# A hybrid decoder layer on one core: a second gate tile projected inside the first three token groups, with the next group's turns spread over more slices

## The chip, the cores and the metric

The kernel runs on one core of one Trainium2 chip. The metric is the device time of one execution in microseconds; lower is better. Several runs of the same kernel are timed and their median is given. One further execution is recorded by the hardware profiler, and all the views below come from it.

## The reference

One decoder layer over 2048 tokens of width 1024, batch 1. The input x is RMS-normalised and modulated (`h`), then projected by one wide matrix into queries, keys, values and gates of two attention branches:

```python
h = rms_norm(x, g_pre) * (1.0 + scale) + shift          # scale, shift, gate from silu(c) @ w_ada + b_ada
qa, ka, va, fa, za, qb, kb, vb, zb = split(h @ w_in)    # 512,512,512,8,512,512,128,128,512 columns
oa = forgetting_attention(qa, ka, va, fa + b_fgate) * silu(za)      # 8 heads, causal, forget-gate bias
ob = sliding_window_sink_attention(rope(qb), rope(kb), vb, sinks) * silu(zb)   # 8 query, 2 key heads, window 128
y = concat([oa, ob]) @ w_out
out = x + gate * rms_norm(y, g_post)
```

## The kernel before, in words

All large products are made of fp16 pairs: each operand is split into a high and a low half, and a product is three matmuls (high-high, high-low, low-high) for every 128 of the 1024 input columns. The tokens are worked on in four groups of 512 (`ci` 0 to 3, `NCH` = 4).

**The stages.** A start (lines 421 to 641) loads w_ada and the first x tiles, computes scale and shift, and from them the per-column factors `Gp` and `Shp` of the normalised x. `Gp` needs a bound over all columns: line 613 makes `bnd`, line 615 its maximum per partition (`bmx`), and lines 617 to 625 carry it over the partitions to `pH`, `Gp` and `Shp`. A prologue then projects the sliding-window keys and values of all four groups and prepares x group by group. The window stage goes through 32 windows of the sliding-window branch, the forgetting attention follows (8 heads, with the remaining projections between its steps), and the output projection ends the kernel.

**Turns.** x of a group is normalised (`squares` on ScalarE, line 372; `root` on VectorE, lines 92 to 106; `normal`, line 382 on ScalarE or 384 on VectorE), and then turned, 128 columns at a time: `turn_x(ci, k)` issues four transposes on TensorE (line 390), then ScalarE scales them by `Gp` and `Shp` (line 396, once or twice), and VectorE makes the low half (lines 400 and 401). The result, `hT[ci]`, is what every projection reads. Eight turns make a group.

**Slices.** Projection work is cut into units that stand in one list, `punits`, by `add(key, units)`. `kb` is the window keys, `vb` the window values, `qb0` to `qb3` the window queries, `zb0` to `zb3` the gates of the window branch (128 columns each), `va` the forgetting values. A unit of `kb`, `qb` or `zb` is three matmuls of 128x512 (line 307); a unit of `vb` is twelve of 128x136 (line 740); eight units are one key for one group. `fill(n)` (line 1024) takes the next n slices and runs, before each, what `events` has for that position. What comes after a product (copies out of PSUM, tanh, rotation) is put off by `after(n, f)` and run at the n-th `tick`, two slices apart in the prologue. Each engine works through its own instructions in order.

**Weights of a key.** When a key is first added, `add` enters eight events for it, so many slices ahead of its first unit: load by a DMA that GpSimd issues (`w_load`, line 205, 42 slices ahead), the maximum on VectorE (`w_max`, line 211, 31), a trip of the maxima through DRAM, again issued by GpSimd (lines 214 and 219, `mx_d` and `mxr`, 31 and 21), the common scale (`w_scale`, line 230, 12), the high half on ScalarE (line 245, 8), the low half on VectorE (line 251, 6 and 4), and the constants (`w_done`, 3). A position below zero becomes the event's number n (line 911), so load and maximum come no later than the slices 0 and 1. The raw weights lie in one of two buffers (`wraw`), the split ones of zb and va in one of two others (`whl`). kb and zb0 hold the raw buffers at first.

**The list before.** For each of the groups 0, 1 and 2: `kb`, `vb`, `zb0`, 24 units, with the eight turns of the next group behind the units of the list `at_` (line 947). Then kb and vb of group 3, qb0 of group 0, zb0 of group 3, qb0 of group 1 and zb1 of group 0. That is the prologue, `N_PRO` = 144 slices. The other 296 slices (14 of `qbs` and 23 of `others`, eight units each) are dealt out to the 32 windows (line 1061). A window is: maxima of the scores on VectorE (line 844), exps on ScalarE (line 855), transposes on TensorE (`turn`, line 864), the product with the values (line 883), and the scores of the next window (line 831), with slices between them.

**Rows that the prediction reads.** `wh_kb` (line 251) is the low half of kb's weights, `tz` a gate tile after its tanh (lines 351 and 347), `junk` the squares of x, `pxb` the transposes in a window, `hT<-in_x_dram` and `xt<-in_x_dram` the loads of x.

Of the kernel before, what the change touches and what calls it, by code (L numbers as in the profile page):

```python
# [24 lines left out]
NCH = S // CH  # L25
# [15 lines left out]
def hybrid_layer(  # L41
# [158 lines left out]
    def w_load(key, pieces, eng=None):  # L200
        width = VB if key == "vb" else P
        raw = (vbw if key == "vb" else wpool).tile([P, KT, width], F32, tag="wraw", name=f"wr_{key}")
        o = 0
        for col0, n in pieces:
            (eng or G).dma_start(raw[:, :, o:o + n], w_in0[:, col0:col0 + n].rearrange("(k p) n -> p k n", p=P))
            o += n
        wq[key] = [raw]

    def w_max(key):
        mx = sm(1, "w_mx")  # L210
        V.tensor_reduce(mx[:], wq[key][0][:], axis=AX.XY, op=ALU.max, apply_absolute_value=True)
        md = mx_d[len(kaps_seen) % 3]
        kaps_seen.append(key)
        G.dma_start(md[:], mx[:])
        wq[key].append(md)

    def w_back(key):
        mxr = mxp.tile([P, P], F32, tag="mxr", name="mxr")
        G.dma_start(mxr[:], wq[key].pop().rearrange("p o -> (p o)").partition_broadcast(P))
        wq[key].append(mxr)  # L220

    def w_scale(key):

        floor = key[:2] == "qk"
        raw, mxr = wq[key]
        if key in first:
            mx2 = mxr
        else:
            mx2 = sm(1, "w_mx2")
            V.tensor_reduce(mx2[:], mxr[:], axis=AX.X, op=ALU.max)  # L230
        pw = sm(1, "w_pw")
        pow2_floor(pw[:], mx2[:], "w_p2")
        if floor:
            V.tensor_tensor(pw[:], pw[:], pfl[:], op=ALU.max)
        sw = sm(1, "w_sw")
        V.reciprocal(sw[:], pw[:])
        V.tensor_scalar(sw[:], sw[:], 2.0 ** 14, None, op0=ALU.mult)
        wq[key] = [raw, pw, sw]

    def w_high(key):  # L240
        raw, pw, sw = wq[key]
        width = VB if key == "vb" else P
        pool = vbw if key == "vb" else wpq if key[0] in "qk" else wpool
        whl = pool.tile([P, 2, KT, width], F16, tag="whl", name=f"wh_{key}")
        A.activation(whl[:, 0], raw[:], AF.Identity, scale=sw[:])
        wq[key].append(whl)

    def w_low(key, part, parts=2):
        raw, pw, sw, whl = wq[key]
        ks = slice(KT * part // parts, KT * (part + 1) // parts)  # L250
        V.scalar_tensor_tensor(whl[:, 1, ks], raw[:, ks], sw[:], whl[:, 0, ks], op0=ALU.mult, op1=ALU.subtract)  # L251
        if part == parts - 1:
            wq[key] = whl
            pws[key] = pw
# [12 lines left out]
    def w_done(key):  # L267

        kind, j = key[:2], key[2:]
        pw = pws[key]  # L270
        if kind == "qk":
            kap = kappa(pw, key)
            scl[key] = col(f"scl_{key}")
            V.tensor_scalar(scl[key][:], kap[:], kap[:], 0.125, op0=ALU.mult, op1=ALU.mult)
            isc[key] = col(f"isc_{key}")
            V.reciprocal(isc[key][:], scl[key][:])
        elif kind == "qb":
            kap = kappa(pw, key)
            scl[key] = col(f"scl_{key}")
            V.tensor_scalar(scl[key][:], kap[:], kaps["kb"][:], 0.125, op0=ALU.mult, op1=ALU.mult)  # L280
        elif kind == "va":
            kaps[key] = kappa(pw, key)
        else:
            czs[key] = col(f"cz_{key}")
            V.tensor_scalar(czs[key][:], pw[:], pH[:], 2.0 ** -29, op0=ALU.mult, op1=ALU.mult)
            n = int(j) + (4 if kind == "zb" else 0)
            V.tensor_tensor(fac8[:, n:n + 1], kaps["vb" if kind == "zb" else f"va{j}"][:], czs[key][:], op=ALU.mult)

    def pieces(key):
        kind, j = key[:2], int(key[2:] or 0)  # L290
        if kind == "vb":
            return [(OFF_VB, P), (OFF_FA, 8)]
        if kind == "qk":
            return [(OFF_QA + j * 64, 64), (OFF_KA + j * 64, 64)]
        return [({"qb": OFF_QB, "kb": OFF_KB, "va": OFF_VA, "za": OFF_ZA, "zb": OFF_ZB}[kind] + j * P, P)]
# [71 lines left out]
    def squares(ci, us=range(4)):  # L367
        if ci not in rstd:
            rstd[ci] = sm(4, "ss"), sm(4, "rst")
        for u in us:  # L370
            junk = hst.tile([P, D], BF16, tag="junk", name="junk", bufs=1)
            A.activation(junk[:], xt[ci * 4 + u], AF.Square, accum_out=rstd[ci][0][:, u:u + 1])

    def root(ci):
        ss, rst = rstd[ci]
        rsqrt_mean(rst, ss[:], 4)

    def normal(ci, us=range(4)):
        for u in us:
            t, r = ci * 4 + u, rstd[ci][1][:, u:u + 1]  # L380
            if ci == 0 or (ci == 1 and u % 2):
                A.activation(xt[t], xt[t], AF.Copy, scale=r)
            else:
                V.tensor_scalar(xt[t], xt[t], r, None, op0=ALU.mult)
# [20 lines left out]
    def turn_x(ci, k):  # L405
        scaled, split = turn(ci, k)
        after(1, scaled)
        after(2, split)
# [309 lines left out]
    def kb_units(ci):  # L718
        cols_ = slice(ci * CH, (ci + 1) * CH)

        def finish(stg):
            for g in range(2):
                for h in range(2):
                    SP.dma_start(kst[g][64 * h:64 * h + 64, :, cols_], stg[64 * g:64 * g + 64, :, :])

        return proj_units("kb", ci, evac_rope(ci, finish, stp))
# [80 lines left out]
    def qb_units(j, ci):  # L807
        def finish(stg):
            ab[j, ci] = stg

        return proj_units(f"qb{j}", ci, evac_rope(ci, finish, None))
# [88 lines left out]
    def add(key, us):  # L900
        if key not in pkeys and key not in ("kb", "vb"):
            at = len(punits) - (24 if key[:2] == "za" else 0)
            for n, (lead, f) in enumerate(((42, lambda: w_load(key, pieces(key))), (31, lambda: w_max(key)),
                                           (21, lambda: w_back(key)), (12, lambda: w_scale(key)),
                                           (8, lambda: w_high(key)), (6, lambda: w_low(key, 0)),
                                           (4, lambda: w_low(key, 1)), (3, lambda: w_done(key)))):
                if key == "zb0":
                    if n >= 3:
                        events.setdefault(n + 9, []).append(f)
                else:  # L910
                    events.setdefault(max(at - lead, n), []).append(f)
        if key not in pkeys:
            pkeys.append(key)
        punits.extend(us)

    events = {}
    others = []
# [5 lines left out]
    def at_slice(n, f):  # L923
        events.setdefault(n, []).append(f)
# [14 lines left out]
    for ci in range(NCH):  # L939
        n0 = len(punits)  # L940
        add("kb", kb_units(ci))
        add("vb", vb_units(ci))
        if ci < 3:
            add(*others[ci])

            mine, punits[n0:] = punits[n0:], []
            at_ = [10, 12, 14, 16, 17, 18, 19, 20] if ci else [12, 14, 16, 17, 18, 19, 20, 21]
            for n, u in enumerate(mine):
                punits.append(u)
                if n in at_:  # L950
                    punits.append(lambda ci=ci, k=at_.index(n): turn_x(ci + 1, k))
            if ci:
                for u in range(4):
                    at_slice(n0 - 9 + 2 * u, lambda ci=ci, u=u: squares(ci + 1, (u,)))
                    at_slice(n0 + 3 + u, lambda ci=ci, u=u: normal(ci + 1, (u,)))
                at_slice(n0 + 2, lambda ci=ci: root(ci + 1))
            at_slice(n0 + 12, lambda ci=ci: spread(ci + 1))
            if ci < 2:
                at_slice(n0 + 12, lambda ci=ci: [load_x(t) for t in range(4 * ci + 8, 4 * ci + 12)])
# [1 line left out]
    at_slice(n0, lambda: open_fox())  # L961
    at_slice(n0 + 8, gates)
    add("qb0", qb_units(0, 0))
    add(*others[3])
    add("qb0", qb_units(0, 1))
    add(*others[4])
    N_PRO = len(punits)
    qbs = [(f"qb{c_ // 4}", qb_units(c_ // 4, c_ % 4)) for c_ in range(2, 16)]
    n_o = 5
    for n, (key, us) in enumerate(qbs):  # L970
        add(key, us)
        lim = 5 + 5 * (n + 1) // 4 if n + 1 < len(qbs) else len(others)
        for key2, us2 in others[n_o:lim]:
            add(key2, us2)
        n_o = lim
# [621 lines left out]
```

## Time and profile before

| | before |
|---|---|
| median of 3 runs | 1220.45 us (1219.6 to 1221.59) |
| profiled execution, span | 1218.0 us |
| TensorE busy | 1164.0 us (96%), 10832 matmuls |
| VectorE busy | 907.5 us (75%) |
| ScalarE busy | 675.5 us (55%) |
| GpSimd busy | 142.1 us (12%) |
| HBM read, written | 71.56 MB, 25.18 MB |

The span goes from the first to the last instruction that the profiler saw on the core; the profiled execution shows no other time of its own, so it is set beside the median of the runs. PE is TensorE's matmuls, PEld its weight loads, DVE is VectorE, ACT ScalarE, POOL GpSimd, SP the engine that issues most DMAs. In a timeline a row has the start in us, the length, engine, line, operation, what is written and what is read, the shape, and in brackets how long the engine stood idle before it and what it waited for. In a list of waits a row has who waited, for whom, the sum in us, how often, and the longest. The granted clock is 1.00 at TensorE's full speed.

### The profile page before, as it was taken

How to read it: one execution, taken by the hardware profiler on the slowest of the kernel's cores; microseconds unless marked ns; L12 is line 12 of the kernel's file. 1: busy time of each engine (PE TensorE's matmuls, PEld its weight loads, DVE VectorE, ACT ScalarE, POOL GpSimd, SP SyncE). 2: the span in 40 equal slices, each digit the busy share in tenths (PEclk: the TensorE clock that was granted, in tenths of full speed). 3: DMA queues.
4: the chain of work that ended last, by engine and by line, in shares of the span. 5: the costliest groups of instructions: out<-in, count | busy, mean ns of one | idle time of the engine just before them, and what ended most of it. 6: DMA issues, size and time to landing. Idle time of an engine off the chain costs nothing.

```text
span 1218.0 us, 27395 instructions
## 1 busy us (share of the span) xinstructions
PE 1164.0 (96%) x10832; PEld 695.9 (57%) x10832; DVE 907.5 (75%) x2268; ACT 675.5 (55%) x1117; POOL 142.1 (12%) x252
## 2 busy tenths in 40 slices
PE   6789999999999999999999999999999979999996
PEld 2457545865558976555555555555555545555553
DVE  6766557676776747688888798878978797666665
ACT  2666445555655452566667666666766778333231
POOL 2011133223232211011010110010000000000000
PEclk9899999999999999999999999999999989999999
DMA  9554332323323322323334323122111135445652
GB/s 325 187 146 139 81 89 79 86 56 103 93 69 86 57 58 52 76 59 84 83 60 84 86 61 79 39 71 49 38 46 42 58 118 186 144 156 190 202 167 81
DMA packets 88036, 120.71 MB, mean 99 GB/s; under 512 B 27836, under 2 KB 63716, under 8 KB 87908
## 3 DMA queue, kind: packets, MB, share of 16 engines
q1 hardware_dynamic: 76932, 85.94, 23.5%
q0 software_dynamic: 10976, 33.03, 11.6%
q8 instruction: 85, 1.39, 0.6%
q14 instruction: 43, 0.35, 0.1%
HBM read 71.56 MB, written 25.18 MB: 79 GB/s over the span
## 4 chain that ended last, share of the span: by engine, by line
PE 77%; DVE 9%; DMA 5%; issue 3%; ACT 2%; SPq 2%; POOL 1%; DVEq 0%; ACTq 0%; POOLq 0%
PE bk L307 29%; PE bk L1405 12%; PE bk L325 7%; PE sta L1256 4%; PE bk L1207 4%; PE sta L1257 4%; PE poa L1282 2%; PE poa L1283 2%; PE poa L1280 2%; PE pxb L864 2%; PE pss L831 2%; PE pob L883 2%; DVE pha L1270 1%; DVE a_m L1210 1%; PE bk L1368 1%
## 5 line engine op out<-in xcount | busy, mean ns | idle before, releaser
L1263 ACT ACTIVATE p<-sta,lift,scl_qk 128x1024 f32<-128x1024 f32 (+2 forms) x160 | 172.0, 1075 | 135.3 <-PE sta L1257 76.8
L307 PE MATMUL bk<-hT,wh_qk 128*128 128x512 f16 x768 | 194.6, 378 | 0.4 <-DVE a_m L1210 0.4
L1405 PE MATMUL bk<-wohl,oz 128*128 128x512 f16 x768 | 172.4, 379 | 1.7 <-ACT wohl L1345 0.8
L1210 DVE TENSOR_REDUCE a_m<-bk 128x1 f32<-128x512 f32 x192 | 130.2, 685 | 52.4 <-PE bk L1207 51.7
L1270 DVE TENSOR_TENSOR pha<-p,pha 128x1024 f16<-128x1024 f32 (+2 forms) x160 | 169.0, 1056 | 0.0
L1267 ACT ACTIVATE pha<-p 128x1024 f16<-128x1024 f32 (+2 forms) x160 | 148.0, 925 | 5.9 <-PE poa L1283 0.9
L1405 PEld LDWEIGHTS <-oz 128*128 128x128 f16 x768 | 74.4, 99 | 83.7 <-issue 1.8
L1280 PE MATMUL poa<-vt,pha 128*128 128x65 f16 x1088 | 117.4, 193 | 2.7 <-DVE ona L1289 2.7
L1283 PE MATMUL poa<-vt,pha 128*128 128x65 f16 x1088 | 117.2, 193 | 1.1 <-DVE pha L1270 1.1
L1282 PE MATMUL poa<-vt,pha 128*128 128x64 f16 x1088 | 117.5, 195 | 0.0
L1256 PE MATMUL sta<-T 128*128 128x512 f16 (+1 forms) x320 | 112.2, 351 | 4.7 <-ACT p L1263 4.6
L307 PEld LDWEIGHTS <-wh_qk 128*128 128x128 f16 x768 | 72.4, 97 | 75.2 <-issue 1.4
L1280 PEld LDWEIGHTS <-pha 128*128 128x128 f16 x1088 | 102.4, 97 | 17.4 <-DVE ona L1289 3.8
L1207 PE MATMUL bk<-T 66*128 66x512 f16 (+2 forms) x320 | 109.9, 350 | 2.0 <-DMA T<-stq 1.5
L1257 PE MATMUL sta<-T 69*128 69x512 f16 (+1 forms) x320 | 111.1, 352 | 0.0
L1282 PEld LDWEIGHTS <-pha 128*128 128x128 f16 x1088 | 101.5, 97 | 11.5 <-issue 0.3
L1283 PEld LDWEIGHTS <-pha 128*128 128x128 f16 x1088 | 101.5, 99 | 1.3 <-DVE pha L1270 1.3
L307 PE MATMUL bk<-hT,wh_za 128*128 128x512 f16 x384 | 99.8, 378 | 0.0
L325 PE MATMUL bk<-wh_va,hT 128*128 128x128 f16 x1536 | 91.0, 219 | 0.6 <-issue 0.6
L307 PE MATMUL bk<-hT,wh_zb 128*128 128x512 f16 x384 | 89.9, 379 | 1.1 <-DVE wh_zb L251 1.1
L325 PEld LDWEIGHTS <-hT 128*128 128x128 f16 x1536 | 87.4, 98 | 5.7 <-issue 3.1
L307 PE MATMUL bk<-hT,wh_qb 128*128 128x512 f16 x384 | 87.2, 379 | 0.0
(491 smaller groups left out, 1886.1 us busy)
## 6 DMA issues: line engine op xcount, KB each, us to landing
wa<-in_w_ada_dram SPq DMA_DIRECT2D x16, 512.0 KB
z_d<-tz POOLq DMA_DIRECT2D x32, 256.0 KB, 3.5
T<-stq SPq DMA_DIRECT2D x128, 64.0 KB
T<-o_d SPq DMA_DIRECT2D x16, 512.0 KB
T<-z_d SPq DMA_DIRECT2D x16, 512.0 KB
xr<-in_x_dram SPq DMA_DIRECT2D x16, 512.0 KB
out_dram<-yg SPq DMA_DIRECT2D x15, 512.0 KB
xt<-in_x_dram SPq DMA_DIRECT2D x12, 512.0 KB
```

The source lines that it names most:

```text
L307: PE.matmul(ps, whl[:, a, k, :], hT[ci][:, b, k, :], start=(k == 0 and n == 0), stop=(k == KT - 1 and n == 2))
L325: PE.matmul(ps[:, u * P:(u + 1) * P], hT[ci][:, a, k, u * P:(u + 1) * P], whl[:, b, k, :], start=(k == 0 and n == 0), stop=(k == KT - 1 an ...
L1207: PE.matmul(mx[:, :w], T[0:XM, 0, i * P:(i + 1) * P], T[0:XM, 2, pc * CH:pc * CH + w], start=True, stop=True)
L1256: PE.matmul(self.st[:, o:o + w], T[:, 3, kb_], T[:, 1, qc], start=True, stop=False)
L1257: PE.matmul(self.st[:, o:o + w], T[0:XR, 2, kb_], T[0:XR, 0, qc], start=False, stop=not diag)
L1263: A.activation(self.p32[:, :self.w], self.st[:, :self.w], AF.Exp, scale=scl[f"qk{self.hd}"][:], bias=lift[:])
L1267: A.activation(self.ph[:, 0, :self.w], self.p32[:, :self.w], AF.Copy)
L1270: V.tensor_tensor(self.ph[:, 1, :self.w], self.p32[:, :self.w], self.ph[:, 0, :self.w], op=ALU.subtract)
L1280: PE.matmul(po[:, u, :], ph[:, 0, pq], vt[:, b, hd, 0:65], start=(self.first and n == 0 and u == 0), stop=False)
L1282: PE.matmul(po[:, u, 0:64], ph[:, 0, pq], vt[:, b, hd, 65:VW], start=False, stop=False)
L1283: PE.matmul(po[:, u, :], ph[:, 1, pq], vt[:, b, hd, 0:65], start=False, stop=(self.last and n == len(self.blocks) - 1))
L1405: PE.matmul(py, self.hl[:, i, k, :], w_slot(8 * j + k)[:, cc], start=(k == 0 and m_ == 0), stop=(k == KT - 1 and m_ == 2))
```

## The change

Two places of the list are changed, and the bounds that follow from them:

```diff
         if ci < 3:
             add(*others[ci])
+            add(*others[NCH + ci])
 
             mine, punits[n0:] = punits[n0:], []
-            at_ = [10, 12, 14, 16, 17, 18, 19, 20] if ci else [12, 14, 16, 17, 18, 19, 20, 21]
+            at_ = [14, 16, 18, 20, 22, 24, 26, 28]
...
     add("qb0", qb_units(0, 0))
-    add(*others[3])
+    add(*others[NCH - 1])
     add("qb0", qb_units(0, 1))
-    add(*others[4])
+    add(*others[2 * NCH - 1])
...
-    n_o = 5
+    n_o = 2 * NCH
...
-        lim = 5 + 5 * (n + 1) // 4 if n + 1 < len(qbs) else len(others)
+        lim = 2 * NCH + n + 1 if n + 1 < len(qbs) else len(others)
```

`others[0:4]` is zb0 and `others[4:8]` is zb1, one entry for each group. So the groups 0, 1 and 2 have 32 units each now (kb, vb, zb0, zb1) and their eight turns stand behind the units 14, 16 and so on to 28, counted from 0; the prologue ends with zb1 of group 3 in the place of group 0, and has 168 slices; the window stage has 272. The computation is the same.

The list is not the only thing that moves. zb1 is now first needed at unit 24 of group 0, so its events fall to the first slices of all. On VectorE this is the place in the start where `bmx` is made; `wr_zb_561` is zb1's raw weights, `w_mx` their maximum:

```order
 L611 SCALAR_TENSOR_TENSOR abss<-shf 128x8
 L613 SCALAR_TENSOR_TENSOR bnd<-absg,abss 128x8
+L211 TENSOR_REDUCE w_mx<-wr_zb_561 128x1
 L615 TENSOR_REDUCE bmx<-bnd 128x1
 L619 TENSOR_REDUCE bm<-bk_134 1x1
```

The maximum of zb1's weights stands between `bnd` and `bmx`; before, it stood far down in the prologue, behind the gate tile of group 2.

On GpSimd, from the last constant mask of the start on, before:

```order
L508 AFFINE_SELECT triu<-ones 128x128
L711 TENSOR_TENSOR qs<-qs,sinT 128x512
L349 DMA z_d<-tz 128x512
L711 TENSOR_TENSOR qs<-qs,sinT 128x512
L349 DMA z_d<-tz 128x512
L205 DMA wr_qb_1195<-in_w_in_dram 128x8x128
```

and now:

```order
L508 AFFINE_SELECT triu<-ones 128x128
L205 DMA wr_zb_561<-in_w_in_dram 128x8x128
L214 DMA mx_d_74<-w_mx 128x1
L219 DMA mxr<-mx_d_74 128x128
L711 TENSOR_TENSOR qs<-qs,sinT 128x512
L349 DMA z_d<-tz 128x512 x2
```

The load of zb1 and the trip of its maxima stand ahead of the first rotation (L711). The load takes over kb's raw buffer and therefore waits for VectorE's line 251 on `wh_kb`.

On ScalarE, in group 0, from the copy of vb's second half on, before (`hf` and `hT1` are the scaled turns, `xt8` to `xt11` the x tiles of group 2):

```order
L748 ACTIVATE vb_558<-bk2_136 128x2x64 x2
L713 ACTIVATE stb_590<-qc_589 128x512
L396 ACTIVATE hT1_105<-px_753,Shp_112,Gp_111 128x512
L396 ACTIVATE hf_758<-px_753,Shp_112,Gp_111 128x512
L396 ACTIVATE hf_775<-px_770,Shp_112,Gp_111 128x512
L372 ACTIVATE junk_788,ss_786<-xt8_664 128x1024
L396 ACTIVATE hT1_105<-px_790,Shp_112,Gp_111 128x512
L396 ACTIVATE hf_795<-px_790,Shp_112,Gp_111 128x512
L372 ACTIVATE junk_803,ss_786<-xt9_666 128x1024
L396 ACTIVATE hf_810<-px_805,Shp_112,Gp_111 128x512
L372 ACTIVATE junk_816,ss_786<-xt10_668 128x1024
```

and now, from zb0's tanh on:

```order
L351 ACT_TABLE_LOAD
L351 ACTIVATE tz_834<-bk0_134,cz_zb0_740 128x512
L372 ACTIVATE junk_848,ss_846<-xt8_680 128x1024
L396 ACTIVATE hf_845<-px_840,Shp_112,Gp_111 128x512
L372 ACTIVATE junk_859,ss_846<-xt9_682 128x1024
L396 ACTIVATE hT1_105<-px_861,Shp_112,Gp_111 128x512
L396 ACTIVATE hf_866<-px_861,Shp_112,Gp_111 128x512
L372 ACTIVATE junk_874,ss_846<-xt10_684 128x1024
L372 ACTIVATE junk_886,ss_846<-xt11_686 128x1024
```

The squares of group 2 began behind the fourth turn of eight and alternated with the rest; now zb0's tanh and its table load come first, the squares begin behind the fifth turn, and the last turn (its row follows) stands behind all four of them.

## The prediction

> **What bounds the kernel now.** I read the page first, then TensorE's waits, then the busy time by stage, then the timelines of the stages that the change touches.
>
> ```profile
> span 1218.0 us, 27395 instructions
> PEclk9899999999999999999999999999999989999999
> ```
>
> The profiled execution has a span of 1218.0 us; the median of the runs is 1220.45, so 2.45 us lie around the span. TensorE (PE) is busy in nearly every slice, and its granted clock is low only in the first ones. The stages after the start, cut at the places where the program goes from one group of matmuls to the next:
>
> ```profile
> 58.70:73.90 15.20, 15.00 (x155) 11.96 (x154) 11.72 (x40) 11.04 (x19) 1.27 (x1) 1.00 0.51 152
> 73.90:81.93 8.03, 5.81 (x25) 2.33 (x24) 3.62 (x6) 8.00 (x13) 0.00 (x0) 1.00 0.54 139
> 81.93:103.17 21.24, 17.62 (x154) 13.90 (x152) 14.21 (x36) 11.28 (x22) 1.94 (x2) 0.84 0.56 174
> 103.17:108.35 5.18, 5.18 (x26) 2.35 (x24) 2.88 (x7) 3.84 (x8) 0.00 (x0) 1.00 0.00 0
> 108.35:126.90 18.55, 16.85 (x154) 13.38 (x152) 15.08 (x38) 10.27 (x18) 4.58 (x6) 0.91 0.47 115
> 132.08:137.76 5.68, 5.68 (x98) 5.68 (x96) 4.01 (x9) 2.08 (x4) 0.54 (x1) 1.00 0.23 53
> 158.71:423.21 264.50, 264.41 (x2966) 178.81 (x2965) 185.82 (x530) 143.33 (x398) 76.43 (x148) 1.00 0.32 80
> ```
>
> Columns: the stretch, its length, busy PE, PEld, DVE, ACT, POOL, then granted clock and DMA. Row 7 is the window stage: PE works for 264.41 of 264.50 us, so a matmul taken out of it shortens it by its own length, as long as nothing else comes up. Rows 1, 3 and 5 are the rest (vb, zb0, eight turns) of token groups 0, 1 and 2: the same work in 15.20, 21.24 and 18.55 us. Rows 2 and 4 are kb of groups 1 and 2: 8.03 and 5.18 us for the same 24 matmuls.
>
> ```profile
> 66.75 0.60 PE L390 MATMUL px<-ident,hT 128*128 128x128 f32 x4
> 67.83 0.60 PE L390 MATMUL px<-ident,hT 128*128 128x128 f32 x4
> ```
>
> One turn and one zb unit between these two starts take 1.08 us, and a unit is 5.18/8 = 0.65, so a turn is 0.43. A group's rest at full speed is vb 5.68 (row 6) + zb 5.18 + 8 x 0.43 = 14.30 us. **The time lost** is then 0.9 (group 0), 2.85 (kb of group 1), 6.94 (group 1) and 4.25 (group 2): 14.9 us.
>
> ```profile
> PE px L390 <- DVE xt L384: 5.3, 8, 2.0
> PE bk L307 <- DVE hT L401: 1.7, 4, 1.0
> PE bk L307 <- DVE wh_zb L251: 1.1, 1, 1.1
> ```
>
> These waits of PE between 56 and 160 us are half of it: turns wait for the normalised x (L384), kb waits for the turned x (L401), and zb1's first unit, at 156.45, waits for its weights (L251). With these 1.1 us the loss is 16.0.
>
> ```profile
> 63.53 1.58 PE L740 MATMUL bk<-wh_vb,hT 128*128 128x136 f16 x24
> 89.35 2.93 PE L740 MATMUL bk<-wh_vb,hT 128*128 128x136 f16 x24
> ```
>
> The other half is the clock: the same 24 matmuls take 1.58 us before and 2.93 us behind the waits of group 1.
>
> **The change part by part.** Moved: zb1's units of groups 1, 2 and 3 leave the window stage; those of groups 0, 1 and 2 are done in their groups, that of group 3 at the end of the prologue. On PE the groups get 3 x 5.18 = 15.5 us longer, and the window stage loses 72 matmuls; at the rate of the window stage, on the chain that ended last:
>
> ```profile
> 203.00 5.93 PE bk L307 x27
> ```
>
> that is 72 x 0.22 = 15.8 us. So 0.3 us is gained, no more; the move pays only by the 16.0 us of waits and lost clock that the matmuls can stand in.
>
> What of the 16.0 stays. A turn now stands two to eight units later in its group, one for two units and not one for each, and three units part the last one from the next kb (two in group 0 before).
>
> ```profile
> 78.44 1.06 ACT L372 ACTIVATE junk<-xt 128x1024 bf16<-128x1024 f32 x1
> 82.30 0.69 DVE L347 SCALAR_TENSOR_TENSOR tz<-tz,bk 128x512 f32<-128x512 f32 x1 [0.85 <-ACT tz L351]
> 85.28 3.75 DVE L384 TENSOR_SCALAR xt<-xt,rst 128x1024 f32<-128x1024 f32 x4
> ```
>
> - kb of group 1 (2.85 now): ACT is busy 11.04 + 8.00 = 19.0 us in rows 1 and 2 and gets 1.8 more (a weight split, a tanh); PE gets to 14.3 + 2 x 5.18 = 24.7. ACT is no longer near the bound. But the last turn's copy now stands behind four squares (L372, 1.06 each and their read-outs), and counted through ACT's queue it comes about 0.4 us late (estimate). I take 0.4.
> - First turn of group 1 (3.6 of the 5.3): DVE's way from tz (L347, 82.30) to the end of the four L384 (89.03) takes 6.7 us. By the same count it starts 4.6 us behind the end of zb1, since zb1's tanh ends ACT's backlog, and so ends 11.3 us behind it. The turn stands 8 units of kb and 7 of vb, 5.2 + 7 x 0.71 = 10.2 us, and the 0.4 behind that end: it waits 0.7 us (estimate). What that does to the clock:
>
> ```profile
> 110.00:112.00 2.00, 0.97 (x13) 0.63 (x10) 1.90 (x6) 0.00 (x0) 0.00 (x0) 1.00 0.80 150
> 112.00:114.00 2.00, 1.33 (x13) 0.94 (x14) 1.84 (x3) 0.33 (x1) 0.00 (x0) 1.00 0.98 298
> 114.00:116.00 2.00, 2.00 (x20) 2.00 (x18) 0.85 (x3) 1.45 (x4) 0.00 (x0) 0.51 0.79 175
> ```
>
> In group 2 four waits of together 1.7 us, with PE busy for more than half the time between them, were enough for 0.51 of the clock; at 0.91 over 18.55 us that cost 1.7 us. I put the same 1.7 to group 1: 2.4 in all. The Trainium skill (TensorE: Matmul & The Clock Gate, Part 1: The HAM clock gate) has the clock halved only after an idle window of some 3.4 us; by that my 0.7 us would cost no clock and the time would be 1.7 us less. This trace disagrees, with the 0.51 behind waits of 1.7 us in which PE was never idle that long.
> - Groups 0 and 2: 0.9 each, what group 0 loses now. zb1's wait for weights goes whole: they are split in group 0.
>
> Left: 0.4 + 2.4 + 1.8 = 4.6 us.
>
> **The price, at the start.** zb1's weights are now loaded into the buffer of kb's, and their maximum is taken on DVE right before L615:
>
> ```profile
> 41.04 1.28 DVE L251 SCALAR_TENSOR_TENSOR wh_kb<-wr_kb,w_sw,wh_kb 128x1024 f16<-128x1024 f32 x1 [0.58 <-ACT wh_kb L245]
> 46.07 0.16 DVE L615 TENSOR_REDUCE bmx<-bnd 128x1 f32<-128x8 f32 x1
> 48.06 0.23 DVE L625 TENSOR_SCALAR Shp<-shf,ipH 128x8 f32<-128x8 f32 x1
> ```
>
> ```profile
> 48.48 0.76 ACT L396 ACTIVATE hT<-px,Shp,Gp 128x512 f16<-128x512 f32 x1
> ```
>
> GpSimd's load must wait for the last reader of kb's raw weights, L251, which ends at 42.32. DVE works in order, so L615, from which Gp, Shp and then every L396 and all of kb come, stands behind a load that is on its way. The same load, later in the program, and its maximum:
>
> ```profile
> 126.36 0.91 POOL L205 DMA_DIRECT2D wr_zb<-in_w_in_dram  x1
> 132.24 1.22 DVE L211 TENSOR_REDUCE w_mx<-wr_zb 128x1 f32<-128x1024 f32 x1 [0.69 <-DMA wr_zb<-in_w_in_dram]
> ```
>
> DVE waited for it until 132.24: 5.9 us from issue. And the queues at the time:
>
> ```profile
> 43.00:44.00 1.00, 1.00 (x11) 1.00 (x10) 0.97 (x2) 0.87 (x3) 0.00 (x0) 1.00 1.09 350
> 44.00:45.00 1.00, 0.93 (x9) 0.69 (x7) 0.96 (x3) 0.87 (x2) 0.00 (x0) 1.00 1.08 176
> 45.00:46.00 1.00, 0.00 (x0) 0.00 (x0) 0.90 (x4) 0.00 (x0) 0.00 (x0) 1.00 0.52 98
> ```
>
> The DMA engines are full of x until 45; the load's descriptors are out at 43.3, so I add half of the 1.7 us, 0.9. Landing at 42.4 + 5.9 + 0.9 = 49.2, the maximum done at 50.4: L615 is **4.3 us late**, and kb, the turns and all behind them with it, for L396 starts at 48.48, 0.2 us behind Shp. Without sharing it is 3.4; if the load gets nothing before the queues are empty at 46, it lands at 51 and the stall is 6.2. The Trainium skill (DMA: Bandwidth & Descriptors, Anatomy of one DMA — SWDGE (gpsimd) path) fits 2.0 us and bytes over 436e3: by that these 512 KB take 3.2 us, and with the 0.91 of issue L615 would be 1.6 us late and the time 2.7 us less (estimate). The trace's 5.9 for the same load decides.
>
> zb1's scale on DVE (L230) comes right behind zb0's:
>
> ```profile
> 63.08 0.15 DVE L237 TENSOR_SCALAR w_sw<-w_sw 128x1 f32<-128x1 f32 x1
> 130.50 0.28 DVE L230 TENSOR_REDUCE w_mx<-mxr 128x1 f32<-128x128 f32 x1 [1.99 <-DMA mxr<-mx_d]
> ```
>
> ```profile
> 117.80 0.76 POOL L214 DMA_DIRECT2D mx_d<-w_mx  x1 [0.51 <-DVE w_mx L211]
> ```
>
> The way over DRAM took 12.7 us there (117.80 to 130.50). From 50.5 it ends at 63.2, against 63.2 + 4.3 = 67.5 when DVE comes to it: 4.3 us of room, no cost.
>
> The window stage loses cover: 24 of 296 slices, 0.5 us in each of 31 windows. The last exp and the turn that needs it, in a usual window and in the tightest:
>
> ```profile
> 198.89 0.19 ACT L855 ACTIVATION_READ_ACCUMULATOR sm__2267<-sm__2267,b_nb 128x1 f32 x1
> 318.77 0.19 ACT L855 ACTIVATION_READ_ACCUMULATOR sm__4181<-sm__4181,b_nb 128x1 f32 x1
> ```
>
> ```profile
> 201.17 1.07 PE L864 MATMUL pxb<-ident,sm__2267 128*128 128x128 f32 x8
> 319.22 0.53 PE L864 MATMUL pxb<-ident,sm__4181 128*128 128x128 f32 x3
> ```
>
> 2.1 us lie between them in the first, 0.26 in the second, 1.2 or more in all others. So one window pays 0.2.
>
> **Sum**: -16.0 + 4.6 + 4.3 - 0.3 + 0.2 = -7.2 us. Span 1218.0 - 7.2 = 1210.8, and with the 2.45 around it 1213.2.
>
> **Rivals.**
> - A, the start hardly stalls: the load moves at the 350 GB/s of the stretch 43 to 44, 1.5 us behind its descriptors, and is there at 44.8. Then L615 waits for the maximum itself alone, 1.2 us: -16.0 + 4.6 + 1.2 - 0.1 = -10.3, 1210.1. For it: DVE has work until 46.07. Against: the 5.9 us. 0.10.
> - B, the waits move instead of going: ACT, 82% busy in rows 1 and 2, stays late from turn to turn, and two thirds of the 14.9 stay. -16.0 + 10.0 + 4.3 - 0.1 = -1.8: 1218.6. For it: one late turn halves the clock for microseconds, as rows 3 and 5 show. Against: the turns are spread over 24.7 us of PE, and group 2 has no squares at all. 0.18.
> - C, slower: the windows are bound by maxima, exps and turns, not by PE, and give nothing back. The first window comes 15.5 - 16.0 + 4.6 + 4.3 = 8.4 us later; without the 15.8 behind it the time is 1228.8. It decides from where less than 53% of the 15.8 comes back, a new wait of 0.24 us in each window. The 0.26 speaks for it, the 1.2 to 2.8 of the other windows against. 0.08.
> - D, the change doesn't do what it says: zb1's weights come too late for group 0, PE stands before its first unit. That needs more than 17 us for the way over DRAM instead of 12.7; each us beyond costs one. Other mishaps with it: 0.06.
>
> **How the numbers follow.** The forecast has the rest, 0.58. The range goes from 1208.5 (between the 3.4 us stall with only the 1.8 of groups 0 and 2 left, 1209.5, and A with the same 1.8, 1207.3) to 1219.0 (B; the 6.2 us stall alone gives 1215.1). It leaves out C, most of D and a part of B: 0.2. 0.2% of the time, 2.4 us, is about what a measurement tells from no change. Faster: nearly all of the forecast (0.56), A (0.10), a third of B (0.06), half of D (0.03): 0.75. Same: 0.14, most of B. Slower: 0.11, C and the rest.
>
> **What would show it.** On DVE a wait for wr_zb right before L615, 3.4 to 6.2 us, the maximum included. The waits for L384 and those for L401 nearly gone, kb of group 1 in under 6 us, groups 1 and 2 in about 20 us each with a clock near 1. The first window's scores at 158.7 + 8.4 = 167.1, and the window stage near 249 us without waits for exps. Wrong would be: no wait at L615, a clock of 0.9 or less in groups 1 and 2, or a window stage over 255 us.

## The result and the profile after

The changed kernel takes 1217.41 us (median of 10 runs, 1215.56 to 1220.91), the kernel before 1220.97 beside it: a ratio of 0.9972, 95% interval 0.9961 to 0.9982. In two later sets of runs, below, the ratio was 0.9982 (0.9969 to 0.9994) and 0.9984 (0.9971 to 0.9996). By these ratios it is faster by 2 to 3.5 us, and not by 7.2. One run in each of the two later sets, of 2411.61 and 1514.78 us, is far slower than all others and is left out of the medians. The profiled execution took 1218.8 us, 2.2 of them around the span.

The page of the changed kernel:

```profile
span 1216.6 us, 27400 instructions
...
PEclk8899999999999999999999999999999989999999
```

The row of the clock differs from the one before in the first slice alone (8 for 9), ahead of the change: slices of 30 us are too coarse for it, and the stages have to be read one by one.

The start is what the forecast said, only longer. On DVE, zb1's maximum and L615 behind it, and PE's wait for that:

```profile
50.15 1.22 DVE L211 TENSOR_REDUCE w_mx<-wr_zb 128x1 f32<-128x1024 f32 x1 [4.99 <-DMA wr_zb<-in_w_in_dram]
51.29 0.15 DVE L615 TENSOR_REDUCE bmx<-bnd 128x1 f32<-128x8 f32 x1
```

```profile
PE bk L617 <- DVE bmx L615: 7.8, 1, 7.8
```

L615 starts at 51.29 instead of 46.07, 5.2 us late. (`bnd` itself came 0.9 us sooner in this execution, 44.99 for 45.87, so L615 stood for 6.1.) The busy times by stage, from one group's kb to the next (columns as before: PE, PEld, DVE, ACT, POOL, granted clock, DMA):

```profile
54.73:84.09 29.36, 28.66 (x215) 18.93 (x215) 25.27 (x70) 24.40 (x38) 2.41 (x3) 0.95 0.47 127
84.09:108.81 24.72, 24.72 (x202) 16.44 (x200) 16.46 (x41) 17.10 (x31) 2.40 (x3) 1.00 0.49 146
108.81:133.53 24.72, 24.72 (x202) 16.43 (x201) 17.55 (x43) 13.65 (x25) 3.84 (x5) 1.00 0.44 113
```

Groups 1 and 2 are as long as their matmuls, 14.30 + 2 x 5.18 = 24.66, at full clock. Everything that was lost there has gone. The window stage, from the first window's scores to the last's, and three stretches of it, each from one window's scores to the next window's (the second, the seventh and the thirtieth):

```profile
164.47:421.33 256.86, 251.08 (x2892) 173.56 (x2892) 182.85 (x528) 140.07 (x395) 75.09 (x145) 0.99 0.36 79
174.21:186.52 12.31, 9.98 (x138) 9.08 (x138) 8.47 (x20) 4.90 (x14) 3.14 (x7) 0.86 0.26 55
218.80:228.68 9.88, 8.18 (x96) 5.62 (x95) 5.65 (x17) 4.79 (x14) 3.72 (x6) 1.00 0.23 36
403.53:413.50 9.97, 8.66 (x153) 8.13 (x153) 4.39 (x14) 4.11 (x12) 3.29 (x7) 1.00 0.79 69
```

The same stretch of the kernel before is 263.74 us long, with PE busy for 263.65:

```profile
158.71:422.45 263.74, 263.65 (x2954) 178.30 (x2954) 185.82 (x530) 142.67 (x397) 75.67 (x146) 1.00 0.33 81
```

So the stage gave back 6.9 us of the 15.8, and now PE stands for 5.8 us in it. In the second stretch lost clock comes on top: PE is busy for 9.98 us at a clock of 0.86 with matmuls that take 8.31 at full clock (run e3 below), so of the 4.0 us that this stretch loses, 2.3 are a wait and 1.7 the clock behind it. PE's longer waits between 40 and 430 us, but for those of the start:

```profile
PE bk L325 <- DVE wh_va L251: 2.3, 1, 2.3
...
PE pob L883 <- DVE ptb L869: 1.4, 1, 1.4
PE pss L831 <- ACT stb L713: 1.3, 1, 1.3
PE pob L883 <- issue: 1.3, 1, 1.3
```

The wait for `stb` comes right before the first window's scores, ahead of the stage; the other three are in it. Those for `wh_va`, `ptb` and `stb` all have to do with one thing, the **rotation** of the window queries and keys. ScalarE copies a product to `qf` (L697), SP issues four copies of 64 KB that exchange its halves into `qs` (L699), GpSimd multiplies `qs` (L711), DVE adds it to the rest (L712), and `stb` is made from that. Around the seventh stretch, on SP, POOL, DVE and PE in turn:

```profile
209.03 3.39 SPq L699 DMA_DIRECT2D qs<-qf  x4
```

```profile
210.67 0.58 POOL L214 DMA_DIRECT2D mx_d<-w_mx  x1 [5.72 <-DVE w_mx L211]
...
220.80 1.27 POOL L711 TENSOR_TENSOR qs<-qs,sinT 128x512 f32<-128x512 f32 x1 [8.18 <-DMA qs<-qf]
```

```profile
222.10 0.69 DVE L712 TENSOR_TENSOR qc<-qc,qs 128x512 f32<-128x512 f32 x1 [7.39 <-POOL qs L711]
```

```profile
227.03 0.82 PE L883 MATMUL pob<-vb,ptb 128*128 128x64 f16 x22 [1.39 <-DVE ptb L869]
```

The copies are all issued at 212.4 (209.03 + 3.39) and have landed only at 220.8. DVE works in order, so L712 holds up the window's maxima and `ptb` behind it, and PE stands before its product. Between the first copies and L711, at 210.67, GpSimd sends out zb2's maximum (`mx_d`, 128 pieces of 4 bytes). The wait for va0's weights comes from a rotation too, by another way. Their maximum goes out just ahead of another rotation's copies, and its read-back stands behind that rotation in POOL's order:

```profile
150.51 0.59 POOL L214 DMA_DIRECT2D mx_d<-w_mx  x1 [4.00 <-DVE w_mx L211]
161.77 1.26 POOL L711 TENSOR_TENSOR qs<-qs,sinT 128x512 f32<-128x512 f32 x1 [10.66 <-DMA qs<-qf]
...
165.23 0.54 POOL L219 DMA_DIRECT2D mxr<-mx_d  x1
```

That the maximum holds these copies too is not shown: where it is moved away (e3, e5 and e10 below), this L711 starts at 160.36 to 161.33, hardly sooner.

The issues of DMAs between 100 and 445 us, KB each and the median time to landing of those whose landing the profile tells:

```profile
o_d<-on POOLq DMA_DIRECT2D x32, 128.0 KB, 2.8
...
mx_d<-w_mx POOLq DMA_DIRECT2D x11, 0.5 KB, 9.8
```

Half a kilobyte takes 9.8 us, 128 KB take 2.8. The profile tells the landing of only one of these eleven writes and of 11 of the 32 stores, which took 2.2 to 8.5. Over the whole of the thirteen profiles of this document it is 80 such writes, of 6.8 to 10.3 us. And the long stores have a pattern: the 27 that GpSimd issued within 4 us behind a write of 4-byte pieces took 6.8 to 8.8 us; the 148 that it issued 8 us or more behind one took 2.2 to 6.6, with a median of 2.7.

In the kernel before, DVE waited at L712 for 9.6 us in all between 160 and 440, and at most for 3.9; now it is 20.4 and 7.4:

```profile
DVE qc L712 <- POOL qs L711: 9.6, 3, 3.9
```

```profile
DVE qc L712 <- POOL qs L711: 20.4, 7, 7.4
```

### The profile page after: what moved, and what is told of

Read it like the earlier page. It is cut to its first block, busy times and chain, and to the rows that moved or that the text cites. A ratio compares the mean times of both kernels' runs of the same rounds, so it can differ in the third digit from the quotient of the medians.

```text
span 1216.6 us, 27400 instructions
## 1 busy us (share of the span) xinstructions
PE 1158.6 (95%) x10832; PEld 693.8 (57%) x10832; DVE 904.4 (74%) x2268; ACT 674.7 (55%) x1117; POOL 142.7 (12%) x252
## 4 chain that ended last, share of the span: by engine, by line
PE 82%; DVE 9%; DMA 5%; issue 2%; ACT 2%; SPq 1%; POOL 0%; DVEq 0%; ACTq 0%; POOLq 0%
PE bk L307 32%; PE bk L1406 13%; PE bk L325 6%; PE sta L1257 4%; PE bk L1208 4%; PE sta L1258 4%; PE poa L1283 2%; PE poa L1284 2%; PE poa L1281 2%; PE pxb L864 2%; PE bk L740 2%; DMA qs<-qf 2%; PE pss L831 2%; PE pob L883 2%; DVE pha L1271 1%
```

## The experiments

**Once more, twice (e1_after_again, e11_after_third).** The changed kernel, unaltered. (The expectations number a stretch by the window whose scores end it: their third and fourth window are the second and third stretch here. The seventh and the thirtieth are the stretches of that number.)

> The changed kernel once more, nothing altered. Theory 1 (two losses belong to the kernel: the stall of L615 behind zb1's maximum, about 6 us, and PE's wait for va0's weights at the third window, about 2 us with as much lost clock; the 9.5 us that the copies to qs took at 152, and the waits for ptb at 227 and at 412, belong to the one execution that was profiled): L615 ends again near 51.3, L325 waits again 2 to 3 us for wh_va, but the copies to qs take 4 to 5 us, no 1.8 us before the first window's scores, and the time is 1216 to 1218. Rival (all of them are the kernel's): every one of these waits is there again, and the time is 1218 to 1219.

> The changed kernel once more, beside the two that follow on the same chip, to set them against. All theories: 1217 to 1221, third and seventh window again about 12 and 10 us, the thirtieth about 10.

Measured: 1220.1 beside 1221.84, and 1219.1 beside 1220.91. The second and the seventh stretch of the first:

```profile
173.77:185.00 11.23, 8.63 (x139) 7.61 (x139) 8.48 (x20) 4.90 (x14) 2.31 (x5) 1.00 0.23 60
...
217.27:227.40 10.13, 8.16 (x96) 5.59 (x96) 5.65 (x17) 4.79 (x14) 3.71 (x6) 1.00 0.23 35
```

The rival holds for the waits: the long copies are no accident of one execution, the losses are the kernel's. Of my first theory the half fell that put them down to one execution. The time of 1220.1 lies above both ranges, but the kernel before is 0.9 us slower in that set too. In e11 the loss at the entry falls otherwise than I expected: the first stretch takes 11.29 and the second 9.62, together 20.9 for 21.0 in e1 and 22.1 above. The seventh and the thirtieth take 10.15 and 9.67.

**zb1's maximum behind kb (e2_zb1_max_late).**

```diff
-                    events.setdefault(max(at - lead, n), []).append(f)
+                    at_n = [0, 6, 14, 18, 20, 22, 24, 25][n] if key == "zb1" else at - lead
+                    events.setdefault(max(at_n, n), []).append(f)
```

> The changed kernel with zb1's maximum taken some five slices later, behind kb of group 0, so that L615 no longer stands behind it; the load stays where it is, and the weights' split moves five slices later too (its first use is slice 29). Theory 1 (the price at the start is DVE's stall): L615 ends near 45.2 instead of 51.3, everything behind it comes 6 us sooner, first window's scores near 157 to 159, time 1217.4 - 6.1 = 1211.3 (1210.5 to 1213). Rival (the load itself slows the tiles of x, which land at 46.9, and the turns of group 0 wait for those): no more than 2 us gained, 1215.4 or more, with waits of ACT or PE for x's tiles between 45 and 55.

Measured: 1217.79, ratio 0.9962 (0.9949 to 0.9976), 2.3 us under the changed kernel in that set of runs. L615 is back at 45.14, and kb starts at 49.57 instead of 54.73, but group 0 takes longer:

```profile
49.57:82.43 32.86, 30.03 (x215) 19.26 (x215) 26.24 (x71) 23.36 (x35) 2.95 (x4) 0.92 0.41 111
```

Of the 5.2 us, 3.5 are lost again in group 0. Part of it was my doing: DVE came to the maximum only at 58.66, and PE waited 2.2 us for zb1's weights. Theory 1 does not hold: the first scores came at 162.35, not at 157 to 159. The gain is of the rival's size, but of its waits there is only one, 1.4 us of ScalarE for a tile of x, until 46.61, and the kernel before has the same one (1.5 us, until 46.33).

**The maximum among the splits (e6_zb1_max_next).**

```diff
         w_low("kb", 0, 1)
+        w_load("zb1", pieces("zb1"))
...
+            if k == 3:
+                w_max("zb1")
...
+                elif key == "zb1":
+                    if n >= 2:
+                        events.setdefault([0, 0, 12, 17, 20, 22, 24, 25][n], []).append(f)
```

> The changed kernel with zb1's load where it is, but its maximum taken among the splits of the turned x in group 0, behind zb0's, so that L615 does not stand behind it and the maximum's way over DRAM still starts about 4 us sooner than in the run that put it behind kb. Theory 1 (the stall of L615 is worth its 6 us, and that run gave 4 of them back in waits for zb1's weights): L615 near 45.2, no wait for wh_zb over 0.5 us, first scores about 5 us sooner than in the changed kernel, time 1217.4 - 5 = 1212.4. Rival (the start is bound by the tiles of x, the turns and their splits, and the stall costs only what stands before them): first scores at most 2.5 us sooner, the time 1215 or more.

Measured: 1216.49, ratio 0.9959 (0.9944 to 0.9973). The three groups:

```profile
49.99:81.09 31.10, 29.41 (x215) 19.10 (x215) 25.97 (x70) 22.88 (x35) 3.16 (x4) 0.93 0.40 113
81.09:107.38 26.29, 25.04 (x201) 16.42 (x200) 17.45 (x43) 18.70 (x34) 2.40 (x3) 1.00 0.49 146
107.38:132.11 24.73, 24.73 (x202) 16.42 (x201) 17.57 (x43) 13.55 (x25) 3.84 (x5) 1.00 0.45 113
```

kb starts 4.7 us sooner, group 3 only 1.4 sooner (132.11 for 133.53); the first scores came at 163.02 for 164.47. Group 0 is 1.7 and group 1 1.6 us longer than in the changed kernel. The rival is nearer by the numbers, but what costs here is the new place of the maximum. DVE and ScalarE:

```profile
55.44 1.21 DVE L211 TENSOR_REDUCE w_mx<-wr_zb 128x1 f32<-128x1024 f32 x1
...
69.70 0.28 DVE L230 TENSOR_REDUCE w_mx<-mxr 128x1 f32<-128x128 f32 x1 [1.36 <-DMA mxr<-mx_d]
```

```profile
71.53 0.63 ACT L716 ACTIVATE stb<-qc 128x512 f16<-128x512 f32 x1 [3.19 <-DVE qc L715]
```

With the maximum among the splits, kb of group 0 takes 10.54 us (49.99 to 60.53) and not 9.41. Its trip over DRAM goes out 7.0 us behind the start of kb; in the changed kernel it goes out 3.1 ahead (51.67 for 54.73). So DVE now waits for it at L230, `qc` of the rotation stands behind DVE, and ScalarE stands 3.2 us for `qc`. ScalarE's last copy for group 1 then comes 4.3 us behind the start of kb and not 2.7, and kb waits. ScalarE and DVE do not catch up while PE stands at the start: in the changed kernel both stand there too, for 4.7 and 5.0 us. What the stall alone costs is not measured, since both runs that take it away pay for the maximum elsewhere.

**The old turns (e4_old_turns).** zb1 moved, the turns not:

```diff
-            at_ = [14, 16, 18, 20, 22, 24, 26, 28]
+            at_ = [10, 12, 14, 16, 17, 18, 19, 20] if ci else [12, 14, 16, 17, 18, 19, 20, 21]
```

> Half of the change alone: zb1 stays in the first three groups, but the turns stand at the slices of the kernel before (behind units 12 to 21 in group 0 and 10 to 20 in groups 1 and 2), so that no turn stands among zb1's last units. Theory A (it is the later, wider spread of the turns that ends the waits): the waits for L384 and L401 come back, the clock in groups 1 and 2 falls under 0.95, the time is 6 us or more above the changed kernel's, 1223.5 or more. Theory B (the eight units more in each group are what gives ACT and DVE the time, the spread adds little): groups 1 and 2 stay under 21 us each, the time is within 2.5 us of 1217.4.

Measured: 1217.72, ratio 0.9966 (0.9951 to 0.9981). Groups 1 and 2:

```profile
85.16:111.23 26.07, 25.38 (x201) 16.46 (x200) 16.02 (x40) 18.26 (x34) 3.36 (x4) 1.00 0.54 162
111.23:135.96 24.73, 24.73 (x201) 16.36 (x200) 16.70 (x41) 11.64 (x20) 4.00 (x5) 1.00 0.38 96
```

Theory B holds (without their kb of 5.18 us, groups 1 and 2 take 20.9 and 19.6). The eight units more do most of it; the wider spread adds 1.1 us in group 0 (85.16 - 54.71 = 30.45 for 29.36), 1.35 in group 1, nothing in group 2, and no difference in the time that the runs can tell.

**va0's weights sooner (e3_va0_early).** The maximum nine slices sooner, the rest five to seven:

```diff
+                    lead = [42, 40, 27, 17, 14, 12, 11, 10][n] if key == "va0" else lead
```

> The changed kernel with va0's weights made ready earlier: maximum nine slices, read-back, scale and split five to seven slices sooner, so that the read-back stands ahead of the rotation on GpSimd and the split ahead of the second window. Theory 1 (the window stage's loss sits at its entry, in the wait for va0's weights): the 2.3 us of L325 and the half clock behind it go, the third window lasts 8.3 instead of 12.3 us, time 1217.4 - 4 = 1213.4 (1212.5 to 1214.5). Rival (the windows are bound by the chain of maxima, exps and turns, and the wait for weights only stands in front of that): the wait comes back as one for stb, sm or ptb in the first three windows, the time is 1216.5 or more.

Measured: 1216.24, ratio 0.9950 (0.9937 to 0.9962), 3.9 us under the changed kernel in that set of runs. The second and the third stretch, and a row of POOL in the third:

```profile
172.81:181.12 8.31, 8.31 (x139) 7.53 (x139) 6.05 (x16) 4.53 (x14) 1.44 (x4) 1.00 0.29 76
181.12:191.12 10.00, 7.84 (x78) 4.83 (x77) 6.17 (x21) 4.23 (x11) 2.81 (x5) 1.00 0.23 38
```

```profile
185.06 0.54 POOL L219 DMA_DIRECT2D mxr<-mx_d  x1 [9.66 <-DMA mx_d<-w_mx]
```

The wait for wh_va is gone, as the theory said, and a wait for ptb stands in the next stretch (10.00 for 7.68), as the rival said: of the 4.0 us, 2.3 are lost again, and the stage is only 1.1 us shorter in the profile (255.79). There GpSimd waits 9.7 us for qb1's maximum to come back, with the rotation queued behind. This row gave the second theory: it is the maxima's writes that hold the copies.

**A narrow and a wide write more (e8_narrow_write, e9_wide_write).** Nobody reads them; the two differ in the width, 1 and 128 columns:

```diff
+    mx_x = dram.tile([P, 1], F32, name="mx_x")
...
                     SP.dma_start(qs[32 * r:32 * r + 32, :], qf[32 * (r ^ 1):32 * (r ^ 1) + 32, :])
+                if pool is None:
+                    G.dma_start(mx_x[:], ident[:, 0:1])
```

> The changed kernel plus one more write in each of the 16 rotations of q: right behind the four copies to qs, GpSimd writes one column of the identity (128 pieces of 4 bytes) to DRAM, which nobody reads. Theory 2 (such a write holds what is queued beside it for 7 to 9 us): the copies to qs take 9 to 12 us in nearly every window, DVE waits for qs at L712 in most of them, the time rises by 10 us or more. Rival (the long trips come from something else, the loading of instructions or the loads of weights): trips as before, the time rises by less than 2 us.

> The same as the run with one more write in each rotation, but of the whole identity, 128 pieces of 512 bytes. Theory 2 (it is the small pieces that hold the queues, not the further write on GpSimd's queue): trips to qs as in the changed kernel, the time within 3 us of it. Rival (any write on that queue holds them): as long as with the column, 10 us or more.

Measured: 1242.47 with the narrow one (two runs; ratio 1.0169, 1.0139 to 1.0198), 1217.30 with the wide one (three runs; 0.9961, 0.9947 to 0.9975). With the narrow write, its issues, DVE's wait (three lines were added, L715 is L712) and a wait of PE:

```profile
mx_x<-ident POOLq DMA_DIRECT2D x16, 0.5 KB, 8.4
```

```profile
DVE qc L715 <- POOL qs L714: 37.2, 8, 9.6
```

```profile
PE bk L326 <- issue: 5.4, 2, 5.2
```

With the wide write:

```profile
mx_x<-ident POOLq DMA_DIRECT2D x16, 64.0 KB, 4.4
```

```profile
DVE qc L715 <- POOL qs L714: 16.9, 5, 7.3
```

The second theory holds in the main: 128 pieces of 4 bytes land after 8.4 us (four landings are told, 7.8 to 10.1), 128 times as many bytes in pieces of 512 after 4.4 (three, 1.9 to 6.5), and only the narrow write makes DVE stand longer for the copies (37.2 us; 20.4 in the changed kernel) and the time 25 us longer. But DVE stood for them at eight rotations, not at most of the sixteen. The Trainium skill (DMA: Bandwidth & Descriptors, Queues, rings and completion order) has the rule for it: a DMA's count on its semaphore is a strongly ordered write, which lands only after all earlier writes of that DMA engine, on whatever queue. The changed kernel agrees: before the seventh stretch the copies were all issued at 212.4 and landed 8.4 us later, with the narrow write issued between them at 210.7. No run tells this rule from DMA engines that are simply kept busy by the small pieces.

**The maxima out of the way (e5_maxima_clear, e10_four_maxima).** Only positions in the list change:

```diff
+                    lead = {'va0': {0: 42, 1: 40, 2: 27, 3: 17, 4: 14, 5: 12, 6: 11, 7: 10}, 'qb1': {1: 26, 2: 16}, 'zb2': {1: 22, 2: 14}}.get(key, {}).get(n, lead)
```

> The changed kernel with three maxima moved away from the rotation's copies: va0 as in the run before (nine slices sooner), qb1's five slices later (its read-back too), zb2's nine slices later. Theory 2 (a maximum's write to DRAM, 128 pieces of 4 bytes, takes 7 to 9 us, and whatever is queued on the DMA engines beside it lands no sooner than it; where it meets the copies to qs, DVE stands at L712 and the maxima of the window behind it): the third, fourth and seventh window last about 8.3, 8.5 and 8.3 instead of 12.3, 8.5 and 9.9, no wait of DVE for qs over 3 us, time 1217.4 - 5.8 = 1211.6, or 5 to 6 us under the changed kernel on the same chip. Rival (the windows are bound by their own chain of maxima, exps and turns): other windows get longer instead, and the time is less than 4 us under the changed kernel's, as in the run that moved va0 alone.

Measured: 1214.48, ratio 0.9938 (0.9922 to 0.9954). The changed kernel did not run beside it; by its ratios of 0.9972 to 0.9984 this is 4 to 5.6 us under it. The copies of the seventh stretch on SP, and L711 and the maximum on POOL:

```profile
205.38 2.87 SPq L699 DMA_DIRECT2D qs<-qf  x4
```

```profile
209.88 1.27 POOL L711 TENSOR_TENSOR qs<-qs,sinT 128x512 f32<-128x512 f32 x1 [2.02 <-DMA qs<-qf]
212.46 0.61 POOL L214 DMA_DIRECT2D mx_d<-w_mx  x1 [1.30 <-DVE w_mx L211]
```

```profile
215.14:222.86 7.72, 7.72 (x96) 5.51 (x96) 4.61 (x14) 4.50 (x13) 2.36 (x5) 1.00 0.73 38
397.70:407.75 10.05, 8.71 (x154) 8.14 (x154) 4.40 (x14) 4.11 (x12) 3.30 (x7) 1.00 0.79 73
164.04:415.58 251.54, 249.15 (x2892) 171.95 (x2893) 184.13 (x528) 139.93 (x395) 73.83 (x144) 1.00 0.36 81
```

From the first copy's issue to L711 it takes 4.5 us instead of 11.8, the seventh stretch lasts 7.72 and the second 8.31, and the stage is 5.3 us shorter than in the changed kernel. In these stretches the windows' own chain is not the bound. Two things came otherwise: DVE still waits for `qs` once for 5.2 us, not under 3, and the third stretch takes 8.46 here and 9.24 and 7.68 in the next two runs, so what qb1's new place is worth is not shown. The thirtieth stretch stays at 10.05. For that one va3's maximum was moved too, `'va3': {1: 37, 2: 27}`:

> The changed kernel with the three maxima moved as before, and va3's six slices sooner too. Theory 2 (in the thirtieth window PE waits 1.3 us for nothing that the profile shows, because the loading of its instructions is held by va3's maximum on its way to DRAM, issued 3 us earlier): that wait goes, the thirtieth window lasts 8.5 instead of 10, and the time is 1.3 us under the run with three, 6 us under the changed kernel. Rival (that wait has to do with the loads of the next weights, 2048 pieces of 256 bytes, issued at 404): it stays, and the time is the same as with three.

Measured: 1213.65, ratio 0.9936 (0.9924 to 0.9949), 5.5 us under the changed kernel beside it. The thirtieth stretch:

```profile
399.34:407.85 8.51, 8.51 (x154) 8.08 (x154) 4.75 (x15) 4.11 (x12) 3.39 (x7) 1.00 0.50 105
```

PE's wait for "issue" is gone and the stretch is 1.5 us shorter. In the time this can't be told from the run with three: in this one execution the third stretch took 9.24 and the eighth 10.07, and PE waited for `ptb`. What PE lacked in those waits no row names. By the Trainium skill (Runtime: NRT & Kernel Launch, Instruction fetch mechanics) an engine's sequencer fetches its code by DMA, in blocks of 16 KiB, mostly unseen. A block held by a narrow write would look like this, and like the 5.2 us above, but no run here shows it.

**All together (e7_both).** The edits of e6 and e10.

> All together: the four maxima moved in the window stage, and zb1's maximum moved behind L615 as in the run that put it behind zb0's. Theory 2 with what the start has shown (of the 5 us that kb starts sooner, 1 to 2.5 are left when the first window comes): first scores near 161.5 to 163, window stage 250 to 251, 2 us under the run with four maxima, 8 us under the changed kernel, about 1211 to 1212. Rival (the first window waits for the rotation's copies at 152 in any case, whatever the start does): the time is that of the run with four maxima within 0.7 us.

Theory 2 holds, with the first scores at 161.93. Measured: **1210.32 us** (1209.71 to 1211.63), ratio 0.9915 (0.9902 to 0.9929) to the kernel before, 8.8 us under the changed kernel beside it: the version that beats both. Its window stage, and DVE's wait at the rotation:

```profile
161.93:411.46 249.53, 248.95 (x2892) 171.94 (x2893) 184.10 (x528) 139.73 (x395) 73.79 (x144) 1.00 0.35 81
```

```profile
DVE qc L715 <- POOL qs L714: 11.5, 6, 4.1
```

Now 14.2 of the 15.8 us come back, and PE stands for 0.6 us in the stage. The five runs lie within 1.9 us of each other, those of the changed kernel within 5.4.

## Why the prediction was wrong, point by point

- **The step that failed** is the one on the way back: "72 x 0.22 = 15.8 us. So 0.3 us is gained, no more", with the one tight window, 0.2, as all that the stage would pay. The matmuls did leave it, but only 6.9 us came back. The second stretch lost 4.0 (12.31 against 8.31 with va0's maximum moved), the seventh 2.2 (9.88 against 7.72), the thirtieth 1.5 (9.97 against 8.51): 7.7 of the 8.9 us. In the second va0's weights come late, with their read-back behind a rotation on GpSimd, and part of the loss is the slow clock behind that wait; in the seventh it is a maximum that holds a rotation's copies; what PE lacks in the thirtieth stays open, though it went with va3's maximum. Of the other 1.2 us, 0.6 fall in the first stretch (9.74 for 9.13 in e2 and e4, where PE does not wait for `stb` there), 0.3 were never to be had (the same 72 matmuls had been priced at 3 x 5.18 = 15.5 us in the groups and at 15.8 in the stage), and 0.3 are not traced. I looked for lost cover in the exps and the turns, where nothing happened by itself. I did not look at where the new order puts the trips of the maxima against the rotation's copies, though the list of DMAs was there to be read. The sign given for it, "a window stage over 255 us", came up: 256.9.
- **The gain of 16.0** was right. kb of group 1 takes 5.18 us, groups 1 and 2 take 24.72 at a clock of 1.00, and zb1's first unit waits for nothing. The spread of the turns, which I had counted with it, does 2.4 us of it; the units do the rest.
- **The residue of 4.6** came out as 0.6: 0.5 in group 0 (its rest takes 19.95 us for 14.30 + 5.18) and 0.1 behind it. The largest term, 2.4 for the first turn of group 1, came to nothing. DVE starts its way 4.6 us behind the end of zb1 as forecast, but ends it 10.3 behind and not 11.3: the four of L384 take 2.74 us and not 3.75. The turn comes at 10.15, so it finds x ready, and with no wait there is no slow clock. That e2 and e6 lose 3.5 and 3.3 us in groups 0 and 1 does not bear the estimate out: in e6 this is the maximum's new place, and in e2 2.2 us of it are the wait for zb1's weights.
- **The stall of 4.3** measured 5.2 at L615 and 5.4 at kb (49.29 to 54.73), inside the bounds of 3.4 and 6.2: zb1's weights landed 8.4 us after their issue, not 6.8. What it costs by itself stays open: with the maximum in its other place group 3 comes 1.4 us sooner, and the time is 3.3 us less between the two best runs (1213.65 and 1210.32; the intervals of their ratios overlap a little).
- **First scores** came at 164.47, not 167.1: 5.4 + 0.6 against 4.3 + 4.6 is 2.9 us less; the wait right before them, 1.3 us for ScalarE's part of `stb`, took a part of that back. With va0's maximum moved it is 1.3 in e5 and 0.2 in e10, so its cause is open.
- **The rivals.** A is out, B too: the waits did go. D is out, zb1's weights were in time. C came nearest, with another cause: it decides where less than 53% of the 15.8 comes back, and 44% did. That the time still fell is owed to the prologue, which came out better than I had it.
- **The time.** With the measured terms the sum is -16.0 + 0.6 + 5.4 + 8.7 (15.5 for the groups less the 6.9) = -1.3, and the two spans differ by 1.4 (1218.0 and 1216.6); the medians differ by 3.6. That 1217.41 lies inside the stated range is luck: its upper part was drawn for waits that move within the groups, which did not happen, and not for the windows.

## What to carry to other kernels

A write of a few bytes per partition to DRAM belongs away from every transfer that an engine waits for in order: list the DMAs of each queue beside each other, before and after a change, and see which ones meet. When work moves from one stage to another, whatever is tied to the position of that work moves too, and is to be looked through in the stage that gets shorter. A run that takes a loss away by moving an instruction also measures the new place of that instruction: follow it there before the difference is read as the price of the loss.

## What the runs showed of the hardware that was not expected

A DMA of 0.5 KB in pieces of 4 bytes to DRAM took 6.8 to 10.3 us to land (80 whose landing the profiles tell), where stores of 128 KB mostly took 2.2 to 2.8. Stores issued within 4 us behind such a write took 6.8 to 8.8 us. In the seventh stretch of the changed kernel SP's copies were there 11.8 us behind their first issue, and 4.5 us with the write moved away. Sixteen such writes cost the kernel about 25 us (two runs of 1238.72 and 1246.22, against 1217.30 with sixteen wide ones in the same set).

Behind a single wait of 2.33 us in the second stretch (175.2 to 177.6) TensorE's granted clock was 0.50 from 178 to 180 us.
